# RMSNorm with SiLU on one core: sixteen loads and sixteen stores on one queue, regrouped into turns of other lengths and partly into transfers of two blocks

## The chip, the cores and the metric

The kernel runs on one core of a Trainium2 chip; the other cores are idle. The metric is the device time of one execution in microseconds (us), as the median of several runs. A profile is one further execution, recorded by the hardware profiler; its span runs from its first to its last instruction, and its own device time is a little longer than its span.

## The reference

The input x is 8 x 1024 x 2048 numbers in float32, seen as 8192 rows of 2048; gamma is 2048 numbers.

```python
rms = np.sqrt(np.mean(x ** 2, axis=-1, keepdims=True) + eps)
out = gamma * x / rms
return (out * (1 / (1 + np.exp(-out)))).astype(np.float32)
```

So x is read once (67.1 MB) and out is written once (67.1 MB), and every row needs a sum of squares before its scaling can begin.

## The kernel before, in words

**Blocks.** The rows are cut into 16 blocks of 512 rows. A block is 4 MiB and lies in SBUF as 128 partitions of 4 rows each, 32 KB in one partition. `view` (line 67) pairs neighbouring blocks: the two blocks of pair q share 1024 rows, partition p owns 8 of them that are neighbours in memory (a run of 64 KB), the even block takes the first half of each run and the odd block the second half. A transfer of one block therefore moves 128 runs of 32 KB that lie 64 KB apart. A transfer of an even block together with its odd neighbour moves 128 runs of 64 KB.

**Slots.** One tile, `ring` (line 56, `xt` in the profile), has six slots of 32 KB in each partition. Block b works in place in slot b % 6: the load writes the slot, the engines rewrite it, the store reads it. So the load of block b must wait until the store of block b-6 has landed.

**The queue.** SP issues all 32 transfers of x and out, one after the other, in the order of the list `QUEUE` (line 13): ('L', b) loads block b, ('S', b) stores it. The list is written by hand: turns of 6 loads, 5 stores, 5 loads, 5 stores, 5 loads, 6 stores. `transfers(done)` (line 83) emits the entries of the list into the program as far as the blocks computed so far allow. A load waits on SP for the landing of the store that frees its slot, a store waits on SP for the last SiLU instruction of its block. Whatever SP waits for, all later entries of the list wait behind it. What is issued lines up in the DMA queue (q1) and is worked off in that order.

**The compute of a block.** ScalarE (ACT) squares rows 0 and 1 of each partition and sums them (line 91), VectorE (DVE) does rows 2 and 3 (line 96). ACT takes the square root (line 107), DVE the reciprocal (line 112) and then one multiplication per row by rstd and gamma (line 117, four instructions). ACT runs SiLU over the block in two halves (line 122), and then `transfers(b)` may emit stores. Square root and SiLU use different tables of ACT, which loads the other one at most changes between them.

**The order of the blocks.** `GROUPS` (line 22) cuts the 16 blocks into the groups 0 to 5, 6 to 10 and 11 to 15. Inside a group the squares of the next block stand ahead of the scaling of this block; the first block of a group starts with nothing ahead of it. In a group that isn't the last one, the squares of the group's last block stand after the SiLU of the block before it. DVE and ACT run their instructions strictly in the order of the program, so that a squares instruction that waits for its load also holds the multiplications of the block before it:

```python
            for b in group[1:-1]:
                if b + 1 < end or end == last:
                    squares(b + 1)
                invert(b)
                multiply(b)
                silu(b)
            if end < last:
                squares(end)
```

Block 15 ends the program: DVE multiplies by gamma (line 163), ACT applies rstd and SiLU row by row (line 165), and SP issues the last store.

Of the kernel before, what the change touches and what calls it, by code (L numbers as in the profile page):

```python
# [1 line left out]

# [4 lines left out]

ACT = mybir.ActivationFunctionType
ALU = mybir.AluOpType

QUEUE = [
    ('L', 0), ('L', 1), ('L', 2), ('L', 3), ('L', 4), ('L', 5),
    ('S', 0), ('S', 1), ('S', 2), ('S', 3), ('S', 4),
    ('L', 6), ('L', 7), ('L', 8), ('L', 9), ('L', 10),
    ('S', 5), ('S', 6), ('S', 7), ('S', 8), ('S', 9),
    ('L', 11), ('L', 12), ('L', 13), ('L', 14), ('L', 15),
    ('S', 10), ('S', 11), ('S', 12), ('S', 13), ('S', 14), ('S', 15),
]  # L20

GROUPS = [range(0, 6), range(6, 11), range(11, 16)]


@with_exitstack
def kernel(
    ctx: ExitStack,
    tc: tile.TileContext,
    x: bass.AP,
    gamma: bass.AP,  # L30
    eps: bass.AP,
    out: bass.AP,
):
    nc = tc.nc
    P = nc.NUM_PARTITIONS
    f32 = mybir.dt.float32
    x2 = x.flatten_outer_dims()
    o2 = out.flatten_outer_dims()
    n, d = x2.shape
    J = 4  # L40
    SLOTS = 6
    nblk = n // (P * J)
    last = nblk - 1

    singles = ctx.enter_context(tc.tile_pool(name="singles", bufs=1))
    small = ctx.enter_context(tc.tile_pool(name="small", bufs=3))
    psum = ctx.enter_context(tc.tile_pool(name="psum", bufs=1, space=bass.MemoryType.PSUM))

    Q = 4
    w = d // Q  # L50
    g = singles.tile([P, d], f32, name="g")
    eps_t = singles.tile([P, 1], f32, name="eps_t")
    ones = singles.tile([P, P], f32, name="ones")
    ring = singles.tile([P, SLOTS * J * d], f32, name="xt")
    junk_a = psum.tile([P, d], f32, name="junk_a")
    junk_v = psum.tile([P, d], f32, name="junk_v")
    sss, rmss, rstds = {}, {}, {}

    def rows(b, j, k):
        at = (b % SLOTS) * J + j  # L60
        return ring[:, at * d:(at + k) * d]

    def row(b, j):
        return rows(b, j, 1)

    def view(t, blocks):

        q = blocks[0] // 2
        both = t[q * 2 * P * J:(q + 1) * 2 * P * J, :].rearrange("(p j) d -> p (j d)", p=P, j=2 * J)
        at = blocks[0] % 2 * J  # L70
        return both[:, at * d:(at + len(blocks) * J) * d]

    todo = list(QUEUE)

    def transfer():
        kind, *blocks = todo.pop(0)
        sb = rows(blocks[0], 0, len(blocks) * J)
        if kind == "L":
            nc.sync.dma_start(out=sb, in_=view(x2, blocks))
        else:  # L80
            nc.sync.dma_start(out=view(o2, blocks), in_=sb)  # L81

    def transfers(done):

        while todo and (todo[0][0] == "L" or todo[0][-1] <= done):
            transfer()

    def squares_scalar(b):
        sss[b] = small.tile([P, J], f32, name="ss")
        for j in range(J // 2):  # L90
            nc.scalar.activation(out=junk_a, in_=row(b, j), func=ACT.Square,  # L91
                                 accum_out=sss[b][:, j:j + 1])

    def squares_vector(b):
        for j in range(J // 2, J):
            nc.vector.tensor_tensor_reduce(  # L96
                out=junk_v, in0=row(b, j), in1=row(b, j), scale=1.0, scalar=0.0,
                op0=ALU.mult, op1=ALU.add, accum_out=sss[b][:, j:j + 1])

    def squares(b):  # L100
        squares_scalar(b)
        squares_vector(b)
        root(b)

    def root(b):
        rms = small.tile([P, J], f32, name="rms")
        nc.scalar.activation(out=rms, in_=sss.pop(b), func=ACT.Sqrt, scale=1.0 / d, bias=eps_t)  # L107
        rmss[b] = rms

    def invert(b):  # L110
        rstd = small.tile([P, J], f32, name="rstd")
        nc.vector.reciprocal(out=rstd, in_=rmss.pop(b))  # L112
        rstds[b] = rstd

    def multiply(b):
        for j in range(J):
            nc.vector.scalar_tensor_tensor(out=row(b, j), in0=row(b, j), scalar=rstds[b][:, j:j + 1],  # L117
                                           in1=g, op0=ALU.mult, op1=ALU.mult)

    def silu(b):  # L120
        for h in range(0, J, 2):
            nc.scalar.activation(out=rows(b, h, 2), in_=rows(b, h, 2), func=ACT.Silu)  # L122
        transfers(b)

    with tc.manual_schedule():
        transfer()
        nc.vector.memset(ones, 1.0)  # L127
        nc.vector.memset(eps_t, float(eps))
        nc.scalar.dma_start(out=g[0:1, :], in_=bass.AP(tensor=gamma.tensor, offset=gamma.offset, ap=[[d, 1], [1, d]]))
        nc.scalar.activation(out=junk_a[:, 0:1], in_=ones[:, 0:1], func=ACT.Square)  # L130
        for c in range(Q):
            cols = slice(c * w, (c + 1) * w)
            nc.tensor.matmul(junk_v[:, cols], ones[0:1, :], g[0:1, cols], start=True, stop=True)  # L133
        transfer()
        nc.vector.tensor_copy(out=g, in_=junk_v)  # L135
        transfers(-1)

        for group in GROUPS:
            first, end = group[0], group[-1]
            squares(first)  # L140
            invert(first)
            multiply(first)
            squares_scalar(first + 1)
            silu(first)
            squares_vector(first + 1)
            root(first + 1)
# [8 lines that stand above are left out]
                invert(end)  # L155
                multiply(end)
                silu(end)


        for j in range(J):  # L160
            if j == J // 2:
                invert(last)
            nc.vector.tensor_mul(out=row(last, j), in0=row(last, j), in1=g)  # L163
        for j in range(J):
            nc.scalar.activation(out=row(last, j), in_=row(last, j), func=ACT.Silu,  # L165
                                 scale=rstds[last][:, j:j + 1])
        transfers(last)


# [1 line left out]
_INS = ['x', 'gamma', 'eps']  # L171
_OUTS = [((8, 1024, 2048), 'float32')]

_NUMBERS = {'eps': 9.999999747378752e-06}


# [26 lines left out]
```

## Time and profile before

| | |
|---|---|
| median of 3 runs | 317.42 us (317.34 to 317.85) |
| profiled execution: device time / span | 318.13 / 316.3 us |
| DVE busy | 224.3 us (71% of the span) |
| ACT busy | 217.9 us (69%) |
| transfers on SP's queue | 32 of 4 MiB, 134.22 MB |
| DMA packets on SP's queue | 4608, of which 4096 carry 32 KB each and the rest 4 bytes each |

How to read it. The page gives the busy time of each engine, the span in 40 equal slices with the share that the DMA engines were busy, and the DMA queues with their packets. The view of waits says who waited how long for whom. The timeline lists instructions in order of time; "SPq ... DMA_DIRECT2D" is the issue of a transfer, not the transfer. The moment of a landing can be read where somebody has waited for it: a load's at the first squares instruction of its block, a store's at the issue of the load that takes over its slot. The stretches of a windows view give the bytes that the DMA engines finished in each stretch.

### The profile page before, as it was taken

What the parts mean: (1) busy time and instruction counts of PE and PEld (TensorE: products, weight loads), DVE (VectorE), ACT (ScalarE), POOL (GpSimd) and SP (SyncE); (2) the same over time, 40 slices, a digit from 0 to 9 for tenths busy, and PEclk for the clock granted to TensorE, in tenths of its full rate; (3) what the DMA queues carried; (4) which work ended last, traced back from release to release, by engine and by line L of the source; (5) the groups of instructions that cost most, each with busy time, mean ns of one, the idle gap of its engine ahead of it and who ended that gap; (6) DMA issues with size and microseconds to landing.
All of it is one profiled execution on the core that took longest, in us unless ns stands there. A gap on an engine that the chain in (4) does not pass through costs nothing.

```text
span 316.3 us, 423 instructions
## 1 busy us (share of the span) xinstructions
PE 7.2 (2%) x8; PEld 2.5 (1%) x8; DVE 224.3 (71%) x147; ACT 217.9 (69%) x142; POOL 0.2 (0%) x4
## 2 busy tenths in 40 slices
PE   6200000000000000000000000000000000000000
PEld 2000000000000000000000000000000000000000
DVE  0679999999949005899999949004799999995000
ACT  1349979999794405599899894404499899999000
POOL 0000000000000000000000000000000000000000
DMA  8999999999999999999999999999999999999996
GB/s 332 410 452 435 427 447 414 385 411 460 402 461 402 460 402 460 414 447 423 439 427 435 443 418 447 418 452 410 460 410 452 414 447 410 452 418 443 427 435 269
DMA packets 4612, 134.24 MB, mean 424 GB/s; under 512 B 513, under 2 KB 513, under 8 KB 513
## 3 DMA queue, kind: packets, MB, share of 16 engines
q1 hardware_dynamic: 4608, 134.22, 98.9%
q14 instruction: 2, 0.02, 0.0%
q10 hardware_dynamic: 2, 0.01, 0.0%
HBM read 67.12 MB, written 67.11 MB: 424 GB/s over the span
## 4 chain that ended last, share of the span: by engine, by line
DVE 58%; DMA 25%; ACT 6%; issue 1%; DVEq 1%; ACTq 1%; SPq 0%
DVE xt L117 37%; DMA xt<-in_x_dram 25%; DVE junk_v L96 19%; ACT xt L122 2%; ACT xt L165 2%; DVE xt L163 1%; ACT L107 1%; DVEq L198 1%; DVE ss L96 1%; ACTq L198 1%; DVE rstd L112 0%; ACT rms L107 0%; SPq L81 0%; ACTq L107 0%; DVEq L96 0%
## 5 line engine op out<-in xcount | busy, mean ns | idle before, releaser
L117 DVE SCALAR_TENSOR_TENSOR xt<-xt,rstd,g 128x2048 f32<-128x2048 f32 x60 | 137.1, 2347 | 0.5
L122 ACT ACTIVATE xt<-xt 128x4096 f32<-128x4096 f32 x30 | 107.6, 3612 | 17.5 <-DVE xt L117 17.4
L96 DVE CUSTOM_DVE_ANT_0 junk_v<-xt 128x2048 f32<-128x2048 f32 x32 | 73.5, 2298 | 40.3 <-DMA xt<-in_x_dram 39.6
L91 ACT ACTIVATE junk_a<-xt 128x2048 f32<-128x2048 f32 x32 | 60.0, 1876 | 52.1 <-DMA xt<-in_x_dram 51.6
L107 ACT ACT_TABLE_LOAD x13 | 16.7, 1283 | 2.6 <-DVE ss L96 2.4
L122 ACT ACT_TABLE_LOAD x13 | 16.7, 1283 | 0.2
L112 DVE RECIPROCAL rstd<-rms 128x4 f32<-128x4 f32 x16 | 2.8, 174 | 14.2 <-ACT rms L107 14.2
L163 DVE TENSOR_TENSOR xt<-xt,g 128x2048 f32<-128x2048 f32 x4 | 9.0, 2280 | 0.0
L135 DVE COPY g<-junk_v 128x2048 f32<-128x2048 f32 x1 | 2.3, 2291 | 9.1 <-PE junk_v L133 9.1
L165 ACT ACTIVATE xt<-xt,rstd 128x2048 f32<-128x2048 f32 x4 | 7.7, 1990 | 0.7 <-DVE rstd L112 0.7
L133 PE MATMUL junk_v<-g,ones 1*128 1x512 f32 x8 | 7.2, 1072 | 2.8 <-DMA g<-in_gamma_dram 2.8
L91 ACT ACTIVATION_READ_ACCUMULATOR junk_a<-xt 128x1 f32 x32 | 6.0, 186 | 0.0
L107 ACT ACTIVATE rms<-ss,eps_t 128x4 f32<-128x4 f32 x16 | 4.8, 297 | 0.3
L96 DVE DVE_READ_ACCUMULATOR2_ANT ss<- 128x1 f32 x32 | 4.5, 140 | 0.0
L133 PEld LDWEIGHTS junk_v<-g,ones 1*128 1x128 f32 x8 | 2.5, 326 | 5.9 <-issue 5.9
L130 ACT ACT_TABLE_LOAD x1 | 1.3, 1283 | 1.3 <-PEq L184 1.3
L127 DVE MEMSET ones<- 128x128 f32 x1 | 0.2, 165 | 0.8 <-PEq L184 0.8
L130 ACT ACTIVATE junk_a<-ones 128x1 f32<-128x1 f32 x1 | 0.2, 174 | 0.0
L184 POOL MEMSET const-bfloat16-1.0<- 128x1 bf16 x1 | 0.1, 102 | 0.0
L184 POOL MEMSET const-uint8-127<- 128x1 uint8 x1 | 0.1, 102 | 0.0
L184 POOL MEMSET const-float32-0.0<- 128x1 f32 x1 | 0.1, 99 | 0.2 <-issue 0.2
L184 POOL MEMSET const-float32-1.0<- 128x1 f32 x1 | 0.1, 99 | 0.0
(1 smaller groups left out, 0.1 us busy)
## 6 DMA issues: line engine op xcount, KB each, us to landing
xt<-in_x_dram SPq DMA_DIRECT2D x16, 4096.0 KB, 43.0
out_dram<-xt SPq DMA_DIRECT2D x16, 4096.0 KB, 28.4
g<-in_gamma_dram ACTq DMA_DIRECT2D x1, 8.0 KB
```

What stands on the lines that cost most here:

```text
L91: nc.scalar.activation(out=junk_a, in_=row(b, j), func=ACT.Square, accum_out=sss[b][:, j:j + 1])
L96: nc.vector.tensor_tensor_reduce(out=junk_v, in0=row(b, j), in1=row(b, j), scale=1.0, scalar=0.0, op0=ALU.mult, op1=ALU.add, accum_out=sss ...
L107: nc.scalar.activation(out=rms, in_=sss.pop(b), func=ACT.Sqrt, scale=1.0 / d, bias=eps_t)
L112: nc.vector.reciprocal(out=rstd, in_=rmss.pop(b))
L117: nc.vector.scalar_tensor_tensor(out=row(b, j), in0=row(b, j), scalar=rstds[b][:, j:j + 1], in1=g, op0=ALU.mult, op1=ALU.mult)
L122: nc.scalar.activation(out=rows(b, h, 2), in_=rows(b, h, 2), func=ACT.Silu)
L130: nc.scalar.activation(out=junk_a[:, 0:1], in_=ones[:, 0:1], func=ACT.Square)
L133: nc.tensor.matmul(junk_v[:, cols], ones[0:1, :], g[0:1, cols], start=True, stop=True)
L135: nc.vector.tensor_copy(out=g, in_=junk_v)
L163: nc.vector.tensor_mul(out=row(last, j), in0=row(last, j), in1=g)
L165: nc.scalar.activation(out=row(last, j), in_=row(last, j), func=ACT.Silu, scale=rstds[last][:, j:j + 1])
L198: with _tile.TileContext(nc) as tc:
```

## The change

The list has 25 entries instead of 32. Three pairs of loads (4 and 5, 8 and 9, 10 and 11) and four pairs of stores (0 and 1, 4 and 5, 8 and 9, 10 and 11) are one transfer of 8 MiB each, with 64 KB in each partition. The turns become 6 loads, 4 stores, 4 loads, 4 stores, 2 loads, 2 stores, 4 loads, 6 stores, counted in blocks. The groups of the compute become 0 to 5, 6 to 9 and 10 to 15, so that a group's start again falls on the start of a turn of loads. Nothing else is changed; behind the list all lines move down by two.

```diff
 QUEUE = [
-    ('L', 0), ('L', 1), ('L', 2), ('L', 3), ('L', 4), ('L', 5),
-    ('S', 0), ('S', 1), ('S', 2), ('S', 3), ('S', 4),
-    ('L', 6), ('L', 7), ('L', 8), ('L', 9), ('L', 10),
-    ('S', 5), ('S', 6), ('S', 7), ('S', 8), ('S', 9),
-    ('L', 11), ('L', 12), ('L', 13), ('L', 14), ('L', 15),
-    ('S', 10), ('S', 11), ('S', 12), ('S', 13), ('S', 14), ('S', 15),
+    ('L', 0), ('L', 1), ('L', 2), ('L', 3), ('L', 4, 5),
+    ('S', 0, 1), ('S', 2), ('S', 3),
+    ('L', 6), ('L', 7), ('L', 8, 9),
+    ('S', 4, 5), ('S', 6), ('S', 7),
+    ('L', 10, 11),
+    ('S', 8, 9),
+    ('L', 12), ('L', 13), ('L', 14), ('L', 15),
+    ('S', 10, 11), ('S', 12), ('S', 13), ('S', 14), ('S', 15),
 ]
 
-GROUPS = [range(0, 6), range(6, 11), range(11, 16)]
+GROUPS = [range(0, 6), range(6, 10), range(10, 16)]
```

## The prediction

> **What bounds the kernel now.** I read the page first: what the DMA engines do over the span, and the queues.
>
> ```profile
> DMA  8999999999999999999999999999999999999996
> GB/s 332 410 452 435 427 447 414 385 411 460 402 461 402 460 402 460 414 447 423 439 427 435 443 418 447 418 452 410 460 410 452 414 447 410 452 418 443 427 435 269
> q1 hardware_dynamic: 4608, 134.22, 98.9%
> ```
>
> The DMA engines are full in every slice but the first and the last, and SP's queue alone accounts for 98.9% of their time, while DVE and ACT are busy for 71% and 69%. The swing from 402 to 460 GB/s is a count of whole packets in short slices. Second, the waits, to see on which side the queue is.
>
> ```profile
> ACT junk_a L91 <- DMA xt<-in_x_dram: 51.6, 6, 17.1
> DVE junk_v L96 <- DMA xt<-in_x_dram: 39.6, 3, 20.8
> SPq L198 <- DMA out_dram<-xt: 22.4, 1, 22.4
> ```
>
> The engines wait for loads, 91.2 us in all, and at the end SP waits 22.4 us for stores long issued. The chain of waits names DVE for 58%, but that is the way back through work the queue had not yet needed. Third, the timeline, for the pace of the queue: where somebody waited for a landing, it shows the moment.
>
> ```profile
> 22.53 1.88 ACT L91 ACTIVATE junk_a<-xt 128x2048 f32<-128x2048 f32 x1 [3.16 <-DMA xt<-in_x_dram]
> ...
> 92.09 0.33 SPq L79 DMA_DIRECT2D xt<-in_x_dram  x1
> 101.75 0.33 SPq L79 DMA_DIRECT2D xt<-in_x_dram  x1
> 111.50 0.33 SPq L79 DMA_DIRECT2D xt<-in_x_dram  x1
> ...
> 121.20 2.30 DVE L96 CUSTOM_DVE_ANT_0 junk_v<-xt 128x2048 f32<-128x2048 f32 x1 [18.22 <-DMA xt<-in_x_dram]
> ...
> 218.13 2.30 DVE L96 CUSTOM_DVE_ANT_0 junk_v<-xt 128x2048 f32<-128x2048 f32 x1 [20.77 <-DMA xt<-in_x_dram]
> ...
> 284.20 0.33 SPq L81 DMA_DIRECT2D out_dram<-xt  x1
> ```
>
> Load 1 has landed at 22.53, stores 2, 3, 4 at 92.09, 101.75 and 111.50, load 6 at 121.20, load 11 at 218.13; the last store (issue 292.55 to 292.88, then the 22.4 us) at some 315.5. From 92.09 to 111.50 two transfers take 19.41, so 9.70 us each; loads 0 to 1 give 9.63, stores 7 to 9 (189.12 to 208.44) 9.66. A block costs the queue **9.68 us in either direction**, and 32 of them 309.8 of the 316.3 us. The remaining 6.5 us are the start and the end and the following three stretches of ten transfers (96.8 us each by the pace), each with one turn from loads to stores: from 22.53 to 121.20 98.7, from 121.20 to 218.13 96.9, from 218.13 to 315.5 97.4. The first such turn costs 1.9, the second 0.1, the third 0.6. The windows show the first one in place.
>
> ```profile
> 12.10:50.90 38.80, 0.00 (x0) 0.00 (x0) 36.24 (x26) 32.13 (x23) 0.00 (x0) 1.00 1.00 432
> 50.90:62.30 11.40, 0.00 (x0) 0.00 (x0) 11.37 (x8) 11.31 (x10) 0.00 (x0) 1.00 1.05 408
> 110.40:158.80 48.40, 0.00 (x0) 0.00 (x0) 35.66 (x25) 31.79 (x23) 0.00 (x0) 1.00 1.00 433
> 158.80:207.20 48.40, 0.00 (x0) 0.00 (x0) 33.86 (x21) 35.61 (x21) 0.00 (x0) 1.00 1.00 433
> ```
>
> The last column is GB/s: 432 for loads, 433 for loads and for stores later, 408 where the first stores follow load 5. A turn from stores to loads costs nothing to be seen: from store 4 to load 6 (111.50 to 121.20) 9.70, from store 9 to load 11 (208.44 to 218.13) 9.69.
>
> **Part 1: does the queue stay full?** As long as it does, block number n in the new list lands when block number n lands now, whatever its name. From the moments above, in steps of 9.7: the 6th 62.4, 8th 82, 9th 92.1, 11th 111.5, 12th 121.2, 14th 140.6, 16th 160, 17th 169.7, 18th 179.4, 20th 198.7, 22nd 218.1, 23rd 227.8, 26th 257.4, 28th 276.8, 29th 286.5, 30th 296.1, 31st 305.8. An entry must be issued before the one ahead of it is through, up to 2.5 us before that lands (1.0 us from the first issue, 0.73, to the first packet, 1.73, plus up to 1.5 from a transfer's last packet on the slowest engine to its landing, my estimate from the first and last packets). The stores, with the compute of the same durations in the new order:
>
> - Stores 0 and 1 as one: block 1 is finished when store 1 is issued now, 51.1; needed 62.4. Blocks 4 and 5 land together at 62.4; DVE comes to the squares of 4 at 61.2, so up to 1 us is lost in the compute. Stores 2 (65) and 3 (79): needed 82 and 92.
> - Stores 4 and 5: block 5 is finished at 107 to 108; needed 140.6.
> - Block 6 lands at 111.5 instead of 121.2. Now DVE's multiplications of 6 end 15.8 after the landing (137.0) and its store is issued at 143.41, 22.2 after; so 134. Needed 160.
> - The squares of 8 stand ahead of the scaling of 7 and wait for the pair, 140.6; queued behind them on DVE are reciprocal and multiplications of 7 and 8, on ACT their SiLU, and on SP store 7. In the present group the squares begin at 141.70 and the store of the block before is issued at 159.33, 17.6 later: store 7 at 158.2, needed 169.7. Multiplications of 8 end at 164; the last block of a group is finished 22.2 after (178.79 to 201.0 now): stores 8 and 9 at 186.3, needed 198.7.
> - Loads 10 and 11 wait on SP behind store 7 and for stores 4 and 5 (160), needed 179.4. Load 12 waits behind stores 8 and 9 (187), needed 218; load 14 for their landing (218.1), needed 237.
> - Blocks 10 and 11 land at 198.7 but the squares of 12 stand ahead of the scaling of 11, 227.8; plus 17.6 is 245.4 for stores 10 and 11, needed 257.4. Then one block every 13.97 us, as now (256.26, 270.23, 284.20): stores 12 to 14 at 259.4, 273.4, 287.3, and 15 at 8.35 more (284.20 to 292.55), 295.7; needed 276.8, 286.5, **296.1**, 305.8.
>
> The tightest is store 14: 8.8 us, 6.3 after the 2.5, and now it is 11.9 (284.20). So the waits added by the pairs cost nothing: the cover is the backlog of the queue. Gone, it would cost what the store is late, 1 us for 1 us.
>
> **Part 2: seven transfers fewer.** Seven merges take away 7 x 128 of the 4096 data packets, if a run of 64 KB goes as one packet: 56 of 256 on each of 16 engines. What such a packet takes no row shows. Nearest are gamma's packet of 8 KB, 307 ns in the trace, and one of 32 KB, 1213: (4 x 307 - 1213)/3 = 5 ns that don't grow with the size. So 56 x 5 = 0.28 us saved; at the other end 0, if the runs are cut again. A packet of 4 bytes that reports a landing takes 9 ns: 7 fewer on an engine are 0.06 at most, 0 if hidden, since the pace of 9.681 in the packet list is 8 x 1.210 already; I take 0.03.
>
> The Trainium skill (DMA: Bandwidth & Descriptors, Where 436 GB/s comes from) has a ceiling of 435.2 GB/s. That speaks against any large gain from longer runs: 134.22 MB would take 308.4 us by it, against 309.8 at the pace of the trace, and the merged share of that 1.4 us, 56 of 256 packets, is 0.3, an estimate.
>
> **Part 3: more turns.** From loads to stores 4 instead of 3, from stores to loads 3 instead of 2. The latter I take at 0 (none is seen above). The price of the former lies between 0.1 and 1.9. The new one stands at 198.7, between the second (160) and the third (257), and nearer to the second, so I take its 0.1.
>
> **Sum:** -0.28 - 0.03 + 0.1 = -0.2. The profiled execution would take 317.9 instead of 318.13, with a span of 316.1 instead of 316.3; it lies 0.7 above the median of the runs, and on the median this gives **317.2**. The bounds alone: -0.28 - 0.06 + 0.1 = -0.24 and +1.9, so 317.2 to 319.3.
>
> **The rivals.**
>
> 1. **The first turn is repaired (faster).** In the trace its loss falls on the last two packets that each engine spends on load 5, at 58.2 and 60.4. In the new list those are one packet of a pair, followed by a pair of stores, and store 0 is issued at 51 instead of 35. If what is lost there depends on the packets or on the issue, up to 1.9 us go; at half of it, 317.2 - 0.95 = 316.3. For it: no row repeats that loss with other packets. Against: I know no reason in the profile.
> 2. **The new turn costs what the first did (slower).** Between loads 10 and 11 and stores 8 and 9, at 198, a loss of 1.9 instead of 0.1: 317.2 + 1.8 = 319.0. For it: short turns with long packets meet there, and the price has been seen once. Against: two of three turns cost far less. It decides from a price of 0.9 us on (0.63 beyond the median of before, and the 0.3 that the merges save).
> 3. **A store comes too late.** Store 14 would have to slip by over 6.3 us; at 8 it costs 1.7, 318.9. The compute's steps are as regular as the list above, so this is unlikely.
> 4. **The runs are cut at 32 KB or less**, so the change doesn't do what it says: 0.28 are not saved, 317.5. It ends within the same bound.
>
> **How the numbers follow.** A measurement of this kernel can tell about 0.2% (0.63 us) from no change. Forecast 0.38 and rival 4 0.08 are within it: same 0.46. Rival 1 with smaller gains of the kind 0.31: faster 0.31. Rival 2 0.20 and rival 3 0.03: slower 0.23. The range goes from a little below rival 1 to rivals 2 and 3, 316.0 to 319.0, and leaves out the full repair and the full sum of the bounds, less than 2 in 10.
>
> **What would show it.** Part 1: SP's queue at 98 to 99%, waits of DVE and ACT for loads of about the same sum, store 14 issued near 287 and store 15 near 296, and no slice under 380 GB/s in the middle. Part 2: the packets of q1 fall from 4608 to 3600 (896 data packets and 112 reports fewer); about 4500 means that the runs are cut. Part 3: load 6 landed near 111.5, and the distance to the first landing of the next turns in steps of 9.7. A landing of load 12 at over 229 would prove me wrong on the new turn, a landing of load 6 at under 110 on the first.

## The result, and the profile after

The changed kernel takes **317.92 us** (median of 22 runs, 317.31 to 319.07) against 317.38 us of the kernel before (22 runs beside them, 317.12 to 318.18). The ratio is 1.0019, 95% interval 1.0010 to 1.0027: a small loss of some 0.5 us (0.6 by the means) where 0.2 us of gain were forecast. Its runs also scatter over 1.8 us, those of before over 1.1. The profiled execution took 319.07 us with a span of 317.3, at the upper end of its runs as that of before (318.13) was.

The page after, in the order in which it was read before: the DMA engines' busy tenths, their GB/s, SP's queue (packets, MB, share of the time of 16 engines).

```profile
DMA  8999999999899999999999999999999999999994
GB/s 332 426 434 454 405 463 405 388 405 513 364 438 443 417 454 405 521 405 397 421 434 454 409 512 405 397 421 438 430 434 438 421 459 405 454 413 446 426 434 207
q1 hardware_dynamic: 3600, 134.22, 98.5%
```

The packets are 3600, as counted in advance: the long runs do go as one packet each. The one 8 in the middle, at 364 GB/s, lies under the 380 that the forecast had set as a limit, but it is no hole: the slice ahead of it shows 513, and the two together 438. These rows and the windows view count a packet whole in the slice in which it begins, not in the one in which it is finished, so that a stretch can show a share over 1 (1.05 in a row above), and packets of 64 KB make the swings larger. In the packet list of the trace no engine stands without work for over 0.1 us behind the first turn, but for the two instruction packets that are told below. The last slice has fallen, from 6 tenths and 269 GB/s to 4 tenths and 207 GB/s: at the end most engines have nothing left to do for longer, and the span is longer all the same. The waits of the engines, and SP's at the end:

```profile
ACT junk_a L93 <- DMA xt<-in_x_dram: 45.8, 7, 13.5
DVE junk_v L98 <- DMA xt<-in_x_dram: 43.5, 6, 17.1
...
SPq L200 <- DMA out_dram<-xt: 19.4, 1, 19.4
```

89.3 us of waits for loads stand against 91.2, and SP still waits 19.4 us for the last store: the compute has not become the bound. Third, the timeline, with the moments at which somebody has waited for a landing.

```profile
111.46 2.30 DVE L98 CUSTOM_DVE_ANT_0 junk_v<-xt 128x2048 f32<-128x2048 f32 x1 [7.15 <-DMA xt<-in_x_dram]
...
140.52 1.88 ACT L93 ACTIVATE junk_a<-xt 128x2048 f32<-128x2048 f32 x1 [5.27 <-DMA xt<-in_x_dram]
...
186.10 0.33 SPq L83 DMA_DIRECT2D out_dram<-xt  x1
...
199.54 2.30 DVE L98 CUSTOM_DVE_ANT_0 junk_v<-xt 128x2048 f32<-128x2048 f32 x1 [17.12 <-DMA xt<-in_x_dram]
...
228.60 1.88 ACT L93 ACTIVATE junk_a<-xt 128x2048 f32<-128x2048 f32 x1 [6.93 <-DMA xt<-in_x_dram]
...
288.27 8.57 SPq L83 DMA_DIRECT2D out_dram<-xt  x2
```

Load 6, the 11th block of the queue, lands at 111.46; loads 8 and 9, the 13th and 14th, at 140.52. Both are where the forecast put them (111.5, 140.6). Stores 8 and 9 are issued at 186.10 (186.3 forecast), store 14 at 288.27 and store 15, the second issue of the last line, at 296.5. But loads 10 and 11, the 20th block, land at 199.54 instead of 198.7, and load 12, the 23rd, at 228.60 instead of 227.8. Between 140.52 and 199.54 there are six blocks: 59.02 us instead of 6 x 9.68 = 58.1. By the packets the slowest engine loses **0.8 us where the queue goes from loads 10 and 11 to stores 8 and 9, the turn that the change adds**, and 0.25 on the way from store 7 to these loads; the long packets give some 0.1 back. From there to the last landing (316.4) the twelve blocks take 116.8, as the last twelve before (198.74 to 315.5); both of these stretches hold a loss of 0.6 to 0.7 at the last turn.

A landing is counted when the last of the 16 DMA engines has reported, so it shows the slowest engine. The trace has the reports of all 16 for every transfer. Of the last store the engine in the middle (the median of the 16) reports at 314.25 before and 314.00 after, the last one at 315.49 before and 316.36 after. So two things have happened. In the middle the queue has become 0.25 us faster, which is the gain that was forecast. At the same time one engine has fallen 2.4 us behind the middle, where it was 1.2.

Some 0.6 us of either lag are older than the later turns and don't come from a turn. Before, the last report of load 5 comes 0.13 us behind the middle, that of store 0 comes 0.72 behind. In between, at 70.40, a packet of 8 KB of the queue that the page calls instruction stands in the packet list, exactly where one engine has a gap of 0.30 us; the next packet of that engine takes 0.36 us longer. The stretch from 70 to 71 us of the kernel before shows it:

```profile
q14 instruction: 1, 0.01, 1.9%
```

Every profile of this case has two of these packets, the first at 69.9 to 71.5 us (81.0 in one), the second on another engine at 84.6 to 95.8. The engine that the first one delays is also the one that loses the most at the later turns of both profiles, before 0.59 us at the last one, after 0.81 at the new one (no other engine over 0.23) and 0.72 at the last.

The windows at the end show that engine alone, kernel before first (last two columns: busy share of the 16 engines, GB/s):

```profile
312.00:314.00 2.00, 0.00 (x0) 0.00 (x0) 0.00 (x0) 0.00 (x0) 0.00 (x0) 1.00 0.65 279
314.00:316.00 2.00, 0.00 (x0) 0.00 (x0) 0.00 (x0) 0.00 (x0) 0.00 (x0) 1.00 0.00 0
```

After:

```profile
312.00:314.00 2.00, 0.00 (x0) 0.00 (x0) 0.00 (x0) 0.00 (x0) 0.00 (x0) 1.00 0.65 279
314.00:316.00 2.00, 0.00 (x0) 0.00 (x0) 0.00 (x0) 0.00 (x0) 0.00 (x0) 1.00 0.04 16
```

Up to 314 the two are alike. Then 16 GB/s for 2 us are one packet of 32 KB, which one engine begins when the other fifteen are through (their last packet ends at 313.97).

### The profile page after: what moved, and what is told of

Its sections match the earlier page's. It is cut to its first block, busy times and chain, and to the rows that moved or that the text cites. A ratio compares the mean times of both kernels' runs of the same rounds, so it can differ in the third digit from the quotient of the medians.

```text
span 317.3 us, 421 instructions
## 1 busy us (share of the span) xinstructions
PE 7.2 (2%) x8; PEld 2.5 (1%) x8; DVE 224.4 (71%) x147; ACT 218.2 (69%) x142; POOL 0.2 (0%) x4
## 4 chain that ended last, share of the span: by engine, by line
DVE 46%; DMA 36%; ACT 7%; issue 3%; DVEq 1%; ACTq 1%; another core or an unknown queue 0%; SPq 0%
DVE xt L119 30%; DMA xt<-in_x_dram 29%; DVE junk_v L98 13%; DMA out_dram<-xt 7%; ACT xt L124 3%; ACT xt L167 2%; DVE xt L165 1%; DVEq L200 1%; ACT junk_a L93 1%; ACTq L200 1%; DVE ss L98 0%; ACT L109 0%; DVE rstd L114 0%; ACT rms L109 0%
```

## The experiments

Two theories stood against each other at first. **A: the turns.** An added turn from loads to stores costs the engine that comes to it last, and the long packets save. **B: the long packets.** Packets of 64 KB let an engine fall behind, and turns are free (in the after profile the largest single loss behind the first turn is a packet of 64 KB that took 3.2 us instead of 2.4). All medians are given against runs of the kernel before on the same chip, in the same series.

**The order alone.** The changed order and groups, every transfer of one block:

```diff
-    ('S', 0), ('S', 1), ('S', 2), ('S', 3), ('S', 4),
-    ('L', 6), ('L', 7), ('L', 8), ('L', 9), ('L', 10),
-    ('S', 5), ('S', 6), ('S', 7), ('S', 8), ('S', 9),
-    ('L', 11), ('L', 12), ('L', 13), ('L', 14), ('L', 15),
+    ('S', 0), ('S', 1), ('S', 2), ('S', 3),
+    ('L', 6), ('L', 7), ('L', 8), ('L', 9),
+    ('S', 4), ('S', 5), ('S', 6), ('S', 7),
+    ('L', 10), ('L', 11),
+    ('S', 8), ('S', 9),
+    ('L', 12), ('L', 13), ('L', 14), ('L', 15),
...
-GROUPS = [range(0, 6), range(6, 11), range(11, 16)]
+GROUPS = [range(0, 6), range(6, 10), range(10, 16)]
```

> The changed order of blocks and its groups, every transfer of one block (32 transfers, 4608 packets). Theory A, the added turn from loads to stores costs: the after profile shows one DMA engine losing about 0.8 us at 196 us, so this kernel takes about 0.8 more than before, 318.2, and has no 0.25 us back from packets. Theory B, the 64 KB packets cost: 317.4 like before. In the trace A expects the slowest engine's landing to step back by about 0.5 to 1 us between load 11 and store 8, B no step.

Measured: 317.67 against 317.36, ratio 1.0015 (1.000 to 1.003), with runs from 317.16 to 319.71. The profile has the step: load 10 lands at 188.97 and load 11 at 199.29, 10.32 us for one block of 9.68, with no packet over 32 KB in the kernel.

```profile
188.97 2.30 DVE L98 CUSTOM_DVE_ANT_0 junk_v<-xt 128x2048 f32<-128x2048 f32 x1 [15.36 <-DMA xt<-in_x_dram]
...
199.29 1.88 ACT L93 ACTIVATE junk_a<-xt 128x2048 f32<-128x2048 f32 x1 [3.90 <-DMA xt<-in_x_dram]
```

Of B that leaves little, but 0.3 is less than A's 0.8. (The runs are spread unevenly; by the means the difference is 0.50.)

**The pairs alone.** The turns and groups of before, six transfers of two blocks:

```diff
-    ('L', 0), ('L', 1), ('L', 2), ('L', 3), ('L', 4), ('L', 5),
-    ('S', 0), ('S', 1), ('S', 2), ('S', 3), ('S', 4),
+    ('L', 0), ('L', 1), ('L', 2), ('L', 3), ('L', 4, 5),
+    ('S', 0, 1), ('S', 2), ('S', 3), ('S', 4),
...
-    ('S', 5), ('S', 6), ('S', 7), ('S', 8), ('S', 9),
-    ('L', 11), ('L', 12), ('L', 13), ('L', 14), ('L', 15),
-    ('S', 10), ('S', 11), ('S', 12), ('S', 13), ('S', 14), ('S', 15),
+    ('S', 5), ('S', 6, 7), ('S', 8, 9),
+    ('L', 11), ('L', 12), ('L', 13), ('L', 14, 15),
+    ('S', 10, 11), ('S', 12), ('S', 13), ('S', 14), ('S', 15),
```

> The turns and groups of before with six transfers of two blocks (loads 4 and 5, 14 and 15; stores 0 and 1, 6 and 7, 8 and 9, 10 and 11). Theory A (turns cost, packets save 5 ns each): 6 x 8 x 5 ns = 0.24 less than before, 317.1 to 317.2. Theory B (64 KB packets cost): slower than before, about 317.9 like the changed kernel.

Measured: 317.26 against 317.36, ratio 0.9996 (0.9987 to 1.0004). Its page and timeline:

```profile
q1 hardware_dynamic: 3744, 134.22, 99.0%
```

```profile
120.89 2.30 DVE L96 CUSTOM_DVE_ANT_0 junk_v<-xt 128x2048 f32<-128x2048 f32 x1 [16.66 <-DMA xt<-in_x_dram]
...
217.79 2.30 DVE L96 CUSTOM_DVE_ANT_0 junk_v<-xt 128x2048 f32<-128x2048 f32 x1 [20.74 <-DMA xt<-in_x_dram]
```

Load 6 lands 0.3 us earlier than before (121.20), load 11 as well (218.13). Long packets by themselves cost nothing here, even around the first and the last turn, so B alone is out. Once more, in another series:

> The kernel of e2_pairs once more (the turns of before, six pairs), to see whether its 0.1 us under before hold: 6 x 8 x 5 ns = 0.24 less than before if packets save 5 ns each, 317.1 to 317.3; 317.4 if that first measurement was chance.

Measured: 317.29 against 317.53, ratio 0.9994 (0.9984 to 1.0004). Twice 0.1 to 0.2 us under before, each time within the interval of no change. Both series together, 22 runs, lie 0.19 us under before on the mean, 0.05 to 0.33 by resampling the runs: the saving of the packets, where no turn is added.

**More turns.** Single transfers, in the middle turns of two; first after the list of before, then shifted by one block, since the one later turn of before that costs nothing goes from an even block to an odd one:

```diff
+    ('S', 0), ('S', 1),
+    ('L', 6), ('L', 7),
+    ('S', 2), ('S', 3),
+    ('L', 8), ('L', 9),
+    ('S', 4), ('S', 5),
+    ('L', 10), ('L', 11),
+    ('S', 6), ('S', 7),
+    ('L', 12), ('L', 13),
+    ('S', 8), ('S', 9),
+    ('L', 14), ('L', 15),
...
+GROUPS = [range(0, 16)]
```

> Single transfers, turns of two in the middle: six turns from loads to stores instead of three, one group of sixteen blocks. Theory A: three more turns at 0.8 each, 317.4 + 2.4 = 319.8 (318.2 if only some turns cost). Theory B: 317.4.

```diff
+    ('S', 0), ('S', 1), ('S', 2),
+    ('L', 6), ('L', 7), ('L', 8),
+    ('S', 3), ('S', 4),
+    ('L', 9), ('L', 10),
+    ('S', 5), ('S', 6),
+    ('L', 11), ('L', 12),
+    ('S', 7), ('S', 8),
+    ('L', 13), ('L', 14),
+    ('S', 9), ('S', 10),
+    ('L', 15),
+    ('S', 11), ('S', 12), ('S', 13), ('S', 14), ('S', 15),
...
+GROUPS = [range(0, 16)]
```

> Six turns from loads to stores as in e3_more_turns, single transfers, one group, but shifted by one block, so that four of the turns go from an even block (first half of each run of 64 KB) to an odd one: 8 to 3, 10 to 5, 12 to 7, 14 to 9; the first still goes from 5 to 0, the last from 15 to 11. Theory N, the number of turns sets the price (0.7 each by e3_more_turns): 319.5. Theory P, only turns from an odd block to an even one cost (the one later turn of before that costs nothing goes from load 10 to store 5): 317.4 to 318.0, and no step of the slowest engine at the four turns.

Measured: 319.51 against 317.36, ratio 1.0054 (1.0038 to 1.0069), and 319.44 against 317.41, ratio 1.0060 (1.0041 to 1.0079). Three turns more cost 2.1 and 2.0 us by the medians, so **0.7 us each** (1.8 and 1.9 by the means, 0.6 each), with packets of 32 KB only. The shift makes no difference: theory P falls, the number counts. The one group changes the order of the compute as well, but in neither trace has an engine a gap of over 0.1 us behind the first turn, other than the 0.3 us for the two instruction packets: the queue is full there too.

**The first turn.** In every profile the first stores cost the engine in the middle 0.9 to 1.3 us, and all 16 lose there (0.97 to 1.48 before). Load 5 and store 0 exchanged:

```diff
-    ('L', 0), ('L', 1), ('L', 2), ('L', 3), ('L', 4), ('L', 5),
-    ('S', 0), ('S', 1), ('S', 2), ('S', 3), ('S', 4),
+    ('L', 0), ('L', 1), ('L', 2), ('L', 3), ('L', 4),
+    ('S', 0),
+    ('L', 5),
+    ('S', 1), ('S', 2), ('S', 3), ('S', 4),
```

> The list of before with load 5 and store 0 exchanged: four turns from loads to stores (4 to 0, 5 to 1, 10 to 5, 15 to 10), single transfers. Every trace so far loses 1.1 to 1.3 us on all engines where the first stores begin. Theory F, it is the first store that costs: about 1.2 us on the median engine at the turn from load 4 to store 0, at most 0.3 at the turn from load 5 to store 1; the time is 317.4 plus one later turn, 317.7 to 318.1. Theory G, it is the turn after a long stretch of loads: less at the first turn, since it comes after five loads, and the rest at the second.

Measured: 318.59 against 317.53, ratio 1.0024 (1.0013 to 1.0035). By the packets the engine in the middle loses some 1.3 us where store 0 begins and 0.1 to 0.2 where store 1 does. So the first turn is dear wherever it stands (theory F), and here one turn more cost 1.1 by the medians and 0.8 by the means, where F had 0.3 to 0.7. Then an early small store, to have the first write elsewhere:

```diff
         nc.scalar.activation(out=junk_a[:, 0:1], in_=ones[:, 0:1], func=ACT.Square)
+        nc.scalar.dma_start(out=view(o2, [last])[:, 0:P], in_=ones)
```

> Before, plus one early store of 64 KB on ScalarE's queue (the tile ones into the first 128 columns of block 15's part of out, which store 15 overwrites at the end, so the result is that of before). Theory F1, the first write to out costs 1.2 us, and whoever writes first pays: the loss appears during load 0 or 1 and is gone where store 0 begins, 317.4 as before (if it falls beside the idle start, down to 316.3). Theory F2, the first turn of all sixteen engines costs it: the loss stays at store 0, and the 64 KB cost 0.15 to 0.3 more, 317.6 to 317.8.

> The kernel of e2_pairs (turns of before, six pairs) with the early store of e10_early_store. F1 with the loss beside the start: 316.1; F1 without: 317.2; F2: 317.4.

Measured: 317.60 against 317.44, ratio 1.0011 (1.0001 to 1.0022), and 317.57, ratio 1.0002 (0.9992 to 1.0012). The loss stays at store 0 (1.0 us in the middle): 414 GB/s in the stretch that has 408 in the profile before and 432 ahead of it.

```profile
50.90:62.30 11.40, 0.00 (x0) 0.00 (x0) 11.37 (x8) 11.31 (x10) 0.00 (x0) 1.00 1.05 414
```

It is not the first write as such. What it is stays open; it is there in all kernels, 1.2 us in the middle before and 1.3 in the changed kernel, and so isn't what sets them apart. A version that beats both kernels clearly did not come of this.

**A late engine.** A further theory, H: a turn takes more from the engine that comes to it last, the later it comes.

```diff
+        nc.scalar.dma_start(out=rows(5, 0, J)[0:1, :], in_=view(x2, [0])[0:1, :])
         nc.scalar.activation(out=junk_a[:, 0:1], in_=ones[:, 0:1], func=ACT.Square)
```

> Before, plus one load of 32 KB for one partition from ScalarE's queue at the start (the first four rows of x into the place that load 5 fills later; the result is that of before). It puts one or a few DMA engines behind by 1.2 us in all. Theory H, a turn from loads to stores takes more from the engine that comes to it last, the later it comes: that engine keeps its lag and loses 0.5 or more at the second and the third turn, 317.4 + 1.2 + 1.0 to 1.5 = 319.6 to 320.1. Theory I, a turn's loss is chance and does not depend on who is late: 317.4 + 0.5 to 1.2 = 317.9 to 318.6, with the loss of the second turn near 0 as in before. If the load is spread over all 16 engines, both expect under 317.6.

Measured: 319.33 against 317.53, ratio 1.0051 (1.0039 to 1.0063). The load runs on one engine, which reports load 0 1.27 us after the middle. At the first turn it loses 0.9 more than the middle; through the second turn its lag stays the same (2.11, then 2.10), and at the third it gains 0.1; at the end it is 2.41. So H falls: the later engine was not hit harder at the later turns. What the traces show is weaker: where one engine clearly loses the most at a later turn, it is in most profiles the one that is last already, by 0.6 us since the first instruction packet. Why stays open. But none of its lag ever came back, in 300 us of a queue with work for everybody. Each engine has its sixteenth of every transfer (225 of the 3600 packets of the changed kernel), and the last one ends the kernel.

**Turns and long packets together.** The medians did not add up: 0.3 for the order alone and -0.1 to -0.2 for the pairs alone against 0.5 for the change, and the changed kernel, run again beside the order alone, was slower still.

> The changed kernel once more, on the same chip as the three others, for a second trace. Theory A expects the slowest DMA engine to lose time again at the turn from loads 10 and 11 to stores 8 and 9 or at the last one, and the median engine to be about 0.25 us ahead of before; theory B expects losses at long packets away from turns too. About 317.9 either way.

Measured: 318.47 against 317.36, ratio 1.0034 (1.0022 to 1.0046). Next, the changed kernel with single transfers at the new turn only:

```diff
-    ('L', 10, 11),
-    ('S', 8, 9),
+    ('L', 10), ('L', 11),
+    ('S', 8), ('S', 9),
```

> The changed kernel with single transfers around the new turn alone (load 10, load 11, store 8, store 9); three pairs of stores and two of loads stay. If the long packets at the new turn make it dearer, this is faster than the changed kernel by 0.3 us or more, 317.4 to 317.6; if the turn alone sets the price, it takes 317.9 like the changed kernel (two merges fewer give back 0.08).

Measured: 318.03 against 317.53, ratio 1.0020 (1.0008 to 1.0032). And on one chip the order alone, the order with only those two transfers of two blocks, and the changed kernel:

> The kernel of e1_turns once more, beside the two that follow. If the added turn alone is the whole loss of the changed kernel, this takes 0.25 us more than the changed kernel (no merges), so 0.8 to 1.1 over before; if e1_turns' 0.3 over before was right, the long packets must add the rest.

> The order of e1_turns with two transfers of two blocks alone, those at the new turn (loads 10 and 11, stores 8 and 9): the counterpart of e8_turn_single. If long packets at that turn make it dearer: 0.3 to 0.8 over e12_turns_again. If not: 0.08 under it (two merges).

> The changed kernel a third time, as the measure for the two others on this chip. Turn alone: 0.25 under e12_turns_again. Long packets dearer at turns: over e12_turns_again and level with e13_turn_long.

Measured against 317.54: 318.03, ratio 1.0021 (1.0008 to 1.0034); 318.47, ratio 1.0027 (1.0014 to 1.0039); 318.69, ratio 1.0030 (1.0017 to 1.0042). The order alone costs; this time 0.5. The medians rise with every long transfer that is added to it instead of falling by 0.25, but the intervals overlap. Taking the two series together (24 runs of the order alone, 19 of the changed kernel) the changed kernel is slower by 0.39 us on the mean, 0.0 to 0.8 by resampling the runs. With the 22 runs of the result as well, and each series against its own runs of before, the changed kernel stands 0.76 over before and the order alone 0.58, a difference of 0.18 (-0.18 to 0.52). So it is shown that the added turn costs, and that the 0.25 us of the packets do not survive beside it; whether long packets make a turn dearer is not settled, and neither is the place where they would do so. By the means one turn more costs 0.5 and 0.7 (the order alone, twice), 0.8 (load 5 and store 0 exchanged) and 0.6 (each of three).

**A slip that shows the third rival.** Under the next label ran another kernel than the text on record describes: the turns and groups of before with ten transfers of two blocks (loads 4 and 5, 8 and 9, 12 and 13, 14 and 15; stores 0 and 1, 2 and 3, 6 and 7, 8 and 9, 10 and 11, 12 and 13). It says nothing on theory N or P.

> Single transfers, one group, four turns from loads to stores: load 4 to store 0, load 8 to store 3, load 11 to store 6, load 15 to store 10. Theory N: 317.4 + 0.7 = 318.1, and the first turn costs all engines 1.1 to 1.3 us as always. Theory P: the first (even to even) and the second (even to odd) are cheap, the third and fourth cost the slowest engine 0.5 each: between 316.2, if the first turn's 1.2 us go, and 317.9, if they stay.

Measured: 326.30 against 317.41, ratio 1.0281 (1.0266 to 1.0296). Its page has holes in the row of the DMA engines where stores come too late:

```profile
DMA  8999999989999999998999979999989988598997
GB/s 324 453 412 428 453 461 445 388 389 453 453 389 445 392 404 440 509 396 388 392 505 396 404 299 461 388 388 485 420 388 517 388 388 388 259 517 388 388 453 323
```

Stores 8 and 9 are issued at 191.25 there, when stores 6 and 7 ahead of them have landed already (190.05). Holes of this kind, at 299 and 259 GB/s, are what the after profile doesn't have: its 364 follows a 513.

To compare the turns themselves, here is what the slowest engine loses at each one (its time for the blocks across the turn less 9.68 us for each, from the packets of the trace; the first turn is left out):

| kernel | turns near 139 or 159 us | the new one, 198 us | the last one, 257 us |
|---|---|---|---|
| before | 0.0 | | 0.6 |
| pairs alone, twice | 0.0, 0.0 | | 0.0, 0.4 |
| early store, without and with pairs | 0.0, 0.0 | | 0.0, 0.0 |
| the changed kernel, three times | 0.1, 0.0, 0.0 | 0.8, 0.4, 0.6 | 0.7, 0.2, 0.6 |
| the order alone, twice | 0.2, 0.0 | 0.8, 0.3 | 0.9, 0.3 |
| the order with a long new turn | 0.2 | 0.4 | 0.0 |
| the changed kernel, new turn of single transfers | 0.2 | 0.5 | 0.7 |

The same program loses 0.4 or 0.8 at the same turn in two executions. That is of the size of the scatter of the runs, and the changed kernel draws once more than before. Turns from stores to loads cost that engine 0.1 at most, but for the 0.25 told above and 0.27 at the same place in the kernel of the last row.

## Why the prediction was wrong

- **Part 1, the queue stays full: right.** Store 14 was forecast for 287.3 and 15 for 295.7; they were issued at 288.3 and 296.5, both well before they were needed (296.1 and 305.8). The landings up to 140.5 are right to 0.1 us. The squares of block 8 and of block 12 wait as described (8.7 us of DVE each), and it costs nothing. The sign for a hole, a slice under 380 GB/s, did show (364), but in packets of 64 KB it was too tight a limit for a count of whole packets.
- **Part 2, the packets: right in the middle.** 3600 packets, and the engine in the middle ends 0.25 us earlier (0.26 and 0.46 in the two other profiles of the changed kernel), where 0.28 + 0.03 less 0.1 were put. That no run of the 64 KB was cut (rival 4) is settled by the count.
- **Part 3, the new turn: the step that failed.** I took 0.1 for its price, "nearer to the second" turn in place. Measured in seven executions it is 0.3 to 0.8, 0.5 on the mean, and 0.6 to 0.7 for each turn by the two kernels with three turns more. The rows had it: the two later turns of before showed 0.1 and 0.6, and I chose the smaller by its place in time, for which no row gave a reason. With 0.5 in the sum, -0.28 - 0.03 + 0.5, the forecast would have been 317.6, on the right side; the other 0.3 up to the 317.92 measured stay open. The sign set for this step, load 12 landing at over 229, didn't show (228.60): it allowed for 1.2 us, and the turn took 0.8 in this profile.
- **The upper bound, 1.9.** It isn't the price of a turn. Of the 1.9 us lost from load 1 to load 6, 1.2 to 1.3 fall on the engine in the middle too, where the first stores begin, and some 0.6 on one engine alone at 70 us, at the instruction packet.
- **What the sum left out.** It treated the engines as one. The gain falls on each engine, the loss on the one that is last, and only the last one counts; what it has lost is not given back. The last turn, which the sum had as unchanged, lost 0.5 on the mean in the three profiles of the changed kernel and in all seven profiles with the new turn; in the seven that have the turn from load 10 to store 5 it lost 0.3, between 0.0 and 1.0. Whether that is an effect or chance can't be told from these.
- **Rivals.** The second, the new turn costs what the first did, had the place and the direction, with 0.5 instead of 1.9: the dear first turn is another kind, it hits all 16 engines and is seen once in every kernel. The first rival, the first turn repaired, is refuted: 1.2 us in the middle before, 1.3 after. The third did not occur in the changed kernel, and the slip shows what it would have looked like.

## What to carry to other kernels

When one DMA queue is full from end to end, ask of a change what it does to the slowest of the 16 engines, not to their mean rate: a report of landing by landing, first and last engine, shows it, and a row of GB/s does not. Here every further change of direction from loads to stores costs the end of the kernel 0.5 to 0.8 us, more than merging seven pairs of transfers can save, so the fewest turns that the slots allow come first, and longer runs after that. Where the trace shows a price several times and it differs, carry the mean and the spread of all into the sum, instead of the row that looks nearest.

## What the runs showed of the hardware

- Packets of 64 KB are taken whole (3600 packets after, 3744 with six pairs) and take 2418 ns, where two of 32 KB take 2 x 1213. In the pace of the queue a block in a long transfer is 0.02 us faster, 5 ns for each merge on an engine, and with the reports 0.25 us for the engine in the middle.
- A lag of one engine was not made up in this full queue: 1.27 us put on one engine in the first 10 us stood undiminished at the end, and the kernel was 1.8 us longer.
- A packet of 8 KB on the instruction queue, 309 ns at 70.40 us before, goes with a delay of 0.66 us on one engine, and every profile has one at 70 to 81 us. In 190 us of full queue before, from store 0 to load 14, the lag of 0.7 us that it leaves stays.
- Turns from stores to loads cost 0.3 us at most on the engine that ends last, later turns from loads to stores 0.0 to 1.0 us, and mostly the most on the engine that is the last from then on. Why one turn of before (load 10 to store 5) was free (under 0.1) in all seven profiles that have it among three or four turns, and why the last one in the same kernels lost between 0.0 and 1.0, stays open.
